# SSD chunk matrix: the scaled C.B product and its combination move from SBUF into a PSUM bank, and the ring of side banks has four instead of five

## The chip, the cores and the metric

The kernel runs on one core of one Trainium2 chip. The metric is device time in microseconds (us) of one execution. The core has five engines: PE (TensorE, matrix products), DVE (VectorE), ACT (ScalarE), POOL (GpSimd) and SP (SyncE, which here only issues DMA transfers). Each engine works through its own instructions in the order of the program; semaphores make it wait for others. SBUF is the working memory. PSUM is the memory into which PE writes; it has eight banks of 128 partitions by 512 float32.

## The reference: what is computed

Two layers are run over 256 context tokens and 1024 latent tokens, ten tiles of 128 tokens in all. In layer 0 one input projection feeds a bidirectional Mamba-2 (SSD) mixer and a convolution module. The change lies in the SSD mixer, which works in chunks of 128 tokens:

```python
acs = jnp.cumsum(dt * a_neg, axis=2)
seg = acs[:, :, :, None] - acs[:, :, None, :]
lmat = jnp.exp(jnp.where(tril[:, :, None, None], seg, -jnp.inf))
xdt = x * dt[..., None]
cb = jnp.einsum("bcign,bcjgn->bcijg", cm, bm)
y_diag = jnp.einsum("bcijg,bcijgr,bcjgrp->bcigrp", cb, lmat, xdt)
...
y_off = jnp.einsum("bcign,bcigr,bcgrpn->bcigrp", cm, jnp.exp(acs), h_in)
```

This is done forwards and backwards for 16 heads in 4 groups of 4, and the two directions are added. For each chunk and head the kernel builds one 128x128 matrix for both directions. With F and B for C.B masked to the lower and the upper triangle, it is (F times dt forward + B times dt backward) times the exponential of the decays; this matrix times x gives y_diag of both directions.

## The kernel before

**Groups.** Layer 0's SSD part is a loop over the head groups g = 0 to 3. For each, PE computes ten z tiles (the gate and dt, 264 columns) and then four conv blocks: the projections of x, B and C, followed by the 4-tap convolution (ACT evicts the bank and applies the first tap, DVE the other taps in L1146, and L1153 ends the activation). After them comes `out_first(mix["B"])`, the first half of the output projection. Matmuls of these are called main matmuls here.

**Chunk steps.** The SSD work of group g is cut into small steps (`ssd_steps`), which the object `sd` (class `Steps`) hands out between the main matmuls of the next group; those of group 3 go between the main matmuls of `out_first`. The order on every engine is thus written out ahead, by weights in a list; nothing is decided at run time but the waits.

The steps of a group are, in order:

- `prep(c)`: three transposes and C.B of chunk c on PE, copied out by ACT;
- `p1(n)`: the backward recursion. PE makes one chunk's state, POOL scales the state before (L869), DVE adds (L870);
- then for each chunk c two half-steps. `sta(c)`: `sb1(c)`, matmuls with the states (128x256) into bank b2 and with the chunk matrix (128x64) into b1; `sfw(c+1)`, the forward state of the next chunk; `sb2y(c)`, in which DVE reads b2 (L959, twice) and then b1 (L961); and `cbg(c+2)`, below. `stb(c)`: `zmul(c)` on POOL (L968 to L970), `sm(c+2)` (L923), masks on POOL (`msk`), decay arguments on DVE (`arg`, L899), and `scc(c-2)`, two transposes copied out by ACT (L988).

`cbg` builds the chunk matrix for four heads: ACT makes four exponentials (L906), then four scaled copies of the masked C.B into `cbd` (L909), and DVE adds the other direction's part in place (L912, four times 128x128). `sm` then multiplies all 512 columns with the exponentials (L923) into `Mt`, which PE reads in `sb1`. `cbd` is 512 columns of SBUF.

**PSUM banks.** `PS[0]` to `PS[7]` are the eight banks. `mm_bank()` goes round the first of them for main matmuls, `sd_bank()` round the others for the side steps. `banks(n)` sets how many the main matmuls have, and the side steps get the rest; `banks(n, a, w)` gives the side steps the w banks from `PS[a]` on. While the chunk steps run, main matmuls have three banks and side steps five, `PS[3]` to `PS[7]`. In group 0 the z tiles run with four and four, and the conv blocks that follow share the five side banks with the layer-norm steps of the convolution module (`lnb`, transposes L322 read by ACT in L716 and L729). The decay steps (`dt_chain2`) take two side banks, read by DVE in L823, L824 and L826. A bank is handed out again without asking whether it has been read; the wait for its reader follows from the order of the program.

Of the kernel before, what the change touches and what calls it, by code (L numbers as in the profile page):

```python
# [81 lines left out]
def build(tc, I, O):  # L82
    nc = tc.nc
    V, S, G, PE, SP = nc.vector, nc.scalar, nc.gpsimd, nc.tensor, nc.sync
    with ExitStack() as ctx:
# [37 lines left out]
        PS = [psall[:, i * 512:(i + 1) * 512] for i in range(8)]  # L123
# [69 lines left out]
        def banks(n, a=None, w=None):  # L193
            nmm[0] = n
            sdr[0] = (n, 8 - n) if a is None else (a, w)
# [128 lines left out]
        with tc.manual_schedule():  # L324
# [4 lines left out]
            def xa(o, n):  # L329
                return X0[:, o:o + n]  # L330
# [432 lines left out]
            tok = xa(0, 5120)  # L763
            Hb = xa(5120, 2560)
            Hf = [xa(7680 + i * 256, 256) for i in range(2)]
            cbd = xa(8192, 512)
            cbfb = xa(8704, 256)
            X2 = [xa(8960 + i * 256, 256) for i in range(2)]
            yt.append(xa(9472, 256))
# [318 lines left out]
            for g in range(4):  # L1088
# [3 lines left out]
                pend = []  # L1092
                W.need(zp[1])
                W.need(zp[1] + 1)
                banks(4 if g == 0 else 3)
                wps = [W.get(zp[0]), W.get(zp[1])]
                for t in range(NT):
                    b = mm_bank()
# [15 lines left out]
                    sd.tick(T256 * ZF)  # L1114
                    if g == 0 and t == 6:
                        sd.flush()
                banks(3)
                sd.settle()
                if g == 0:
                    lnb_pre()  # L1120
# [539 lines left out]
            for n in range(16 * 7):  # L1660
                g, j = n // 7, n % 7
# [254 lines left out]
```

## Time and profile before

| | |
|---|---|
| median of 3 runs | 2115.37 us (2112.26 to 2115.81) |
| the profiled execution | 2115.44 us, its span 2113.6 us |
| mean granted clock of PE | 0.985 |
| busy: PE, DVE, POOL, ACT | 2024.7, 1364.4, 1034.1, 941.2 us |
| middle and last chunks of groups 0, 1, 2, 3 | from 572 to 655, 710 to 792, 846 to 922 and 1005 to 1064 us |

The span runs from the first to the last instruction that the profile shows; 1.8 us of the time lies around it. Busy times overlap between engines. In rows of the profile a buffer's name is that of its pool: `ps` is a PSUM bank, `X`, `Fhi` and `Flo` are parts of SBUF. `out<-in` names what an instruction writes and reads; the number in brackets behind a row of the timeline is the idle time of its engine before it, and the instruction that ended it.

### The profile page before, as it was taken

The page shows a single profiled execution, that of the slowest core. Times are in us where ns is not written, and L with a number is a line of the kernel's source. Part 1 is how long each engine was busy: PE and PEld are TensorE (multiplying, and loading weights), DVE is VectorE, ACT ScalarE, POOL GpSimd, SP SyncE. Part 2 cuts the span into 40 slices and gives each one's busy share as a digit, 9 for nine tenths or more (in the row PEclk, how much of TensorE's full clock was granted, in tenths as well). Part 3 has the DMA queues.
Part 4 walks back from the last instruction along what each step waited for, and adds up shares of the span by engine and source line. Part 5 has one row for each costly group of instructions (what it writes and reads, how often), then busy time and mean ns, then how long its engine had stood idle before and what let it go on. Part 6 is the DMA issues. An engine that isn't in the chain of part 4 may idle for free.

```text
span 2113.6 us, 32253 instructions
## 1 busy us (share of the span) xinstructions
PE 2024.7 (96%) x12152; PEld 1792.9 (85%) x12152; DVE 1364.4 (65%) x1918; ACT 941.2 (45%) x1768; POOL 1034.1 (49%) x990
## 2 busy tenths in 40 slices
PE   7999999988989989899999999999999999989998
PEld 5778888877968869789998788889999999988987
DVE  5777888878696996985846632235555555564566
ACT  3555565557555554554644432224333333230221
POOL 3488778934554654634714422333444444435412
PEclk9999999999999999899999999999999999999999
DMA  8333321266423323334477643353223233274642
GB/s 340 108 125 130 123 100 66 88 177 191 136 80 95 100 86 103 104 115 155 146 262 228 205 135 125 110 149 112 90 92 95 96 95 95 64 254 163 200 139 81
DMA packets 177620, 283.05 MB, mean 134 GB/s; under 512 B 14432, under 2 KB 119848, under 8 KB 177464
## 3 DMA queue, kind: packets, MB, share of 16 engines
q1 hardware_dynamic: 133728, 239.12, 34.9%
q10 hardware_dynamic: 43736, 41.86, 5.8%
q8 instruction: 96, 1.57, 0.3%
q14 instruction: 60, 0.49, 0.1%
HBM read 206.30 MB, written 74.63 MB: 133 GB/s over the span
## 4 chain that ended last, share of the span: by engine, by line
PE 45%; DVE 8%; DMA 2%; POOL 2%; issue 2%; ACT 1%; ACTq 0%; SPq 0%; DVEq 0%; POOLq 0%
PE ps L207 45%; DVE X L912 2%; DVE Fhi L1146 1%; DVE Fhi L1289 1%; DVE Rl L318 1%; DVE Fhi L899 1%; ACT Rh L317 0%; DMA y2D<-Fm 0%; POOL X L863 0%; DVE Fhi L1290 0%; DVE Fhi L1288 0%; DVE Flo L683 0%; DMA Fhi<-mBD 0%; DVE Wr L259 0%; ACT Fhi L1295 0%
## 5 line engine op out<-in xcount | busy, mean ns | idle before, releaser
L207 PE MATMUL ps<-Rh,Wr 128*128 128x512 f32 (+2 forms) x2944 | 772.2, 348 | 3.1 <-ACT Rh L413 1.4
L207 PEld LDWEIGHTS ps<-Rh,Wr 128*128 128x128 f32 x2944 | 521.2, 192 | 67.4 <-issue 6.2
L207 PE MATMUL ps<-Rl,Wr 128*128 128x256 f32 x1472 | 501.2, 345 | 1.8 <-DVE Rl L415 1.7
L207 PE MATMUL ps<-Wr,Rh 128*128 128x264 f32 (+2 forms) x1812 | 411.0, 318 | 5.9 <-ACT Fhi L1108 2.3
L594 POOL TENSOR_TENSOR X<-X 128x1295 f32<-128x1295 f32 x96 | 297.3, 3097 | 77.8 <-ACT X L592 72.3
L207 PEld LDWEIGHTS ps<-Wr,Rh 128*128 128x128 f32 x1812 | 298.9, 189 | 31.3 <-ACT Fhi L1108 2.5
L207 PEld LDWEIGHTS ps<-Rl,Wr 128*128 128x128 f32 x1472 | 281.2, 192 | 29.8 <-DVE Rl L415 2.7
L207 PE MATMUL ps<-Wr,Rl 128*128 128x264 f32 (+2 forms) x946 | 300.0, 317 | 0.9 <-DVE Rl L318 0.8
L207 PEld LDWEIGHTS ps<-Wr,Rl 128*128 128x128 f32 x946 | 178.7, 189 | 14.4 <-DVE Rl L318 1.3
L207 PE MATMUL ps<-Xa,Rh 128*128 128x512 f32 (+1 forms) x582 | 172.7, 369 | 1.3 <-DVE Xa L259 0.8
L207 PE MATMUL ps<-Xb,Rh 128*128 128x512 f32 (+1 forms) x598 | 170.6, 359 | 0.1
L588 DVE SCALAR_TENSOR_TENSOR ps<-Fhi,Flo,ps 128x1295 f32<-128x1295 f32 x102 | 160.0, 1569 | 2.9
L259 DVE TENSOR_TENSOR Wr<-Flo,Wr 128x1024 fp32r<-128x1024 f32 (+1 forms) x67 | 105.2, 1577 | 54.7 <-ACT Wr L257 54.5
L207 PE MATMUL ps<-Xa,Rl 128*128 128x512 f32 (+1 forms) x342 | 127.1, 372 | 7.1 <-DVE Rl L318 7.1
L1459 ACT ACTIVATE Wr<-Flo 128x512 fp32r<-128x512 f32 x96 | 59.8, 624 | 142.8 <-PE ps L207 141.5
L207 PEld LDWEIGHTS ps<-Xa,Rh 128*128 128x128 f32 x582 | 106.1, 192 | 20.2 <-DVE Xa L259 1.1
L1460 DVE TENSOR_TENSOR Wr<-Flo,Wr 128x512 fp32r<-128x512 f32 x96 | 96.5, 1005 | 39.3 <-ACT Wr L1459 39.3
L207 PEld LDWEIGHTS ps<-Xb,Rh 128*128 128x128 f32 x598 | 105.2, 188 | 17.7 <-DVE Xb L259 0.5
L207 PE MATMUL ps<-S,Wr 128*128 128x256 f32 (+1 forms) x768 | 117.7, 309 | 0.0
L1146 DVE SCALAR_TENSOR_TENSOR Fhi<-Fhi,Flo 128x256 f32<-128x256 f32 (+2 forms) x144 | 113.7, 790 | 4.4
L207 PEld LDWEIGHTS ps<-S,Wr 128*128 128x128 f32 x768 | 110.8, 188 | 0.0
L592 ACT ACTIVATE X<-Fhi,Flo 128x1295 f32<-128x1295 f32 x78 | 103.5, 1373 | 13.4 <-ACT Fhi L641 7.5
(279 smaller groups left out, 3421.5 us busy)
## 6 DMA issues: line engine op xcount, KB each, us to landing
Fhi<-abD SPq DMA_DIRECT2D x80, 256.0 KB, 3.4
Fhi<-in_ada SPq DMA_DIRECT2D x34, 512.0 KB, 7.9
Flo<-in_wug SPq DMA_DIRECT2D x32, 512.0 KB, 4.8
Flo<-in_wB SPq DMA_DIRECT2D x24, 512.0 KB, 3.3
vD<-Flo ACTq DMA_DIRECT2D x40, 256.0 KB, 2.3
Xb<-vD SPq DMA_DIRECT2D x16, 640.0 KB, 5.1
pD<-Xb SPq DMA_DIRECT2D x32, 320.0 KB, 2.5
Flo<-in_wA SPq DMA_DIRECT2D x16, 512.0 KB, 3.5
```

What stands on the lines that cost most here:

```text
L207: PE.matmul(out=out, lhsT=a, rhs=b, start=st, stop=sp)
L259: e.tensor_tensor(out=l_, in0=r, in1=h_.bitcast(F32), op=SUB)
L318: eng.tensor_tensor(out=rl, in0=src, in1=rh.bitcast(F32), op=SUB)
L588: V.scalar_tensor_tensor(out=aD[:, 0:n], in0=u[:, k:k + n], scalar=wc(k), in1=aD[:, 0:n], op0=MULT, op1=ADD)
L592: S.activation(out=o[:, 0:n], in_=u[:, k:k + n], func=AF.Copy, scale=wc(k))
L594: G.tensor_tensor(out=aP[:, 0:n], in0=aP[:, 0:n], in1=o[:, 0:n], op=ADD)
L899: V.scalar_tensor_tensor(out=a[:, q], in0=a[:, q2], scalar=nA[:, sl(1, c)][:, h:h + 1], in1=a[:, q], op0=ADD, op1=MIN)
L912: V.scalar_tensor_tensor(out=cbd[:, q], in0=cbfb[:, 128:256], scalar=dt[:, sl(1, c)][:, h:h + 1], in1=cbd[:, q], op0=MULT, op1=ADD)
L1146: V.scalar_tensor_tensor(out=ob[:, a:e], in0=ib[:, a + k:e + k], scalar=w4(k), in1=ob[:, a:e], op0=MULT, op1=ADD)
L1289: V.tensor_tensor(out=y[:, s_], in0=y[:, s_], in1=grow[:, s_], op=MULT)
L1459: S.activation(out=w[:, 0:512], in_=src, func=AF.Copy)
L1460: V.tensor_tensor(out=w[:, 512:1024], in0=src, in1=w[:, 0:512].bitcast(F32), op=SUB)
```

## The change

`cbd` becomes `PS[7]`. While the chunk steps run, the side steps go round four banks, `PS[3]` to `PS[6]`, and the main matmuls keep their three. Group 0's z tiles keep four and four; so does everything behind the chunk steps of group 3, by a later `banks(4)`.

```diff
             Hf = [xa(7680 + i * 256, 256) for i in range(2)]
-            cbd = xa(8192, 512)
+            cbd = PS[7]
...
                 W.need(zp[1] + 1)
-                banks(4 if g == 0 else 3)
+                if g == 0:
+                    banks(4)
+                else:
+                    banks(3, 3, 4)
                 wps = [W.get(zp[0]), W.get(zp[1])]
...
                     if g == 0 and t == 6:
                         sd.flush()
-                banks(3)
+                banks(3, 3, 4)
                 sd.settle()
```

Every engine has the same instructions in the same order as before; what differs is where some of them read and write, and what they wait for. On DVE, the second half of one chunk in group 0 stood so (`X_92` and `Fhi` are SBUF, the names behind "waits" are the engines waited for):

```order
L961 TENSOR_TENSOR X_92<-X_92,ps 128x256
L912 SCALAR_TENSOR_TENSOR X_92<-X_92,Flo 128x128 [waits DVE_49,Activation_49]
L912 SCALAR_TENSOR_TENSOR X_92<-X_92,Flo 128x128 [waits Activation_49] x3
L1105 SCALAR_TENSOR_TENSOR Fhi<-Fhi,ps 128x256 [waits Activation_49]
L1111 TENSOR_TENSOR Fhi<-ps,Flo 128x2x4
L923 TENSOR_TENSOR Fhi<-Fhi,X_92 128x512 [waits DVE_49]
```

and stands now so:

```order
L961 TENSOR_TENSOR X_92<-X_92,ps 128x256
L912 SCALAR_TENSOR_TENSOR ps<-X_92,Flo,ps 128x128 [waits DVE_49,Activation_49]
L912 SCALAR_TENSOR_TENSOR ps<-X_92,Flo,ps 128x128 [waits DVE_49] x3
L1108 SCALAR_TENSOR_TENSOR Fhi<-Fhi,ps 128x256 [waits Activation_49]
L1114 TENSOR_TENSOR Fhi<-ps,Flo 128x2x4
L923 TENSOR_TENSOR Fhi<-Fhi,ps 128x512 [waits DVE_49]
```

Each of the four L912 waited for its own L909 on ACT; now the first waits for the last L909, since a wait concerns the whole bank, and the others for the L912 ahead (`DVE_49`).

On PE, at `sb1` of a middle chunk of group 1, behind the two transposes of the half-step before, it was:

```order
L322 MATMUL ps<-Flo 128x128 [waits DVE_49,Activation_49]
L322 MATMUL ps<-Flo 128x128
L207 MATMUL ps<-X_92,Fhi 128x256 [waits Activation_49]
L207 MATMUL ps<-X_92,Fhi 128x256 [waits Pool_49]
L207 MATMUL ps<-X_92,Fhi 128x64 [waits DVE_49]
```

and is now:

```order
L322 MATMUL ps<-Flo 128x128 [waits Activation_49]
L322 MATMUL ps<-Flo 128x128
L207 MATMUL ps<-X_92,Fhi 128x256 [waits DVE_49]
L207 MATMUL ps<-X_92,Fhi 128x256 [waits Pool_49]
L207 MATMUL ps<-X_92,Fhi 128x64 [waits Activation_49]
```

The wait for DVE's read of an old bank (L961) has moved from the transposes to the first matmul of the next half-step, one chunk nearer to that read.

## The prediction

> **What bounds the kernel now.** I read the engine totals first, then the stretches in which the chunk steps run, then who waits there.
>
> ```profile
> PE 2024.7 (96%) x12152; PEld 1792.9 (85%) x12152; DVE 1364.4 (65%) x1918; ACT 941.2 (45%) x1768; POOL 1034.1 (49%) x990
> PE 45%; DVE 8%; DMA 2%; POOL 2%; issue 2%; ACT 1%; ACTq 0%; SPq 0%; DVEq 0%; POOLq 0%
> ```
>
> TensorE (PE) is busy 96% of the span, and the chain that ended last is mostly PE, with VectorE (DVE) second. That is an average. The stretches of the chunk steps of head groups 0, 1, 2 and 3 read so (columns: window, its length, busy PE, PEld, DVE, ACT, POOL, granted PE clock, DMA share, GB/s):
>
> ```profile
> 571.71:654.73 83.02, 73.43 (x377) 61.44 (x376) 78.88 (x161) 49.37 (x131) 47.65 (x82) 0.94 0.28 88
> 710.25:791.70 81.45, 69.13 (x365) 59.03 (x364) 79.48 (x159) 49.37 (x131) 50.17 (x79) 0.94 0.28 88
> 845.54:921.65 76.11, 66.16 (x332) 56.91 (x331) 72.66 (x149) 43.86 (x122) 46.76 (x79) 0.89 0.31 100
> 1004.67:1063.60 58.93, 58.83 (x470) 57.55 (x469) 46.16 (x92) 34.39 (x104) 40.87 (x66) 1.00 0.46 150
> ```
>
> In the first three DVE is busy 95 to 98% and PE 85 to 88%: there DVE sets the pace. In the fourth PE is busy all the time and DVE 78%: there each microsecond for which PE stands still is a microsecond of the kernel. The change makes DVE cheaper and PE wait earlier, so the two kinds of stretch answer differently.
>
> One DVE-bound chunk of group 1 (columns: start, length, engine, line, what, count, idle before in brackets):
>
> ```profile
> 742.05 0.41 DVE L961 TENSOR_TENSOR X<-X,ps 128x256 f32<-128x256 f32 x1
> 749.29 0.68 DVE L923 TENSOR_TENSOR X<-Fhi,X 128x512 f32<-128x512 f32 x1
> 749.89 1.13 DVE L899 SCALAR_TENSOR_TENSOR Fhi<-Fhi,Flo 128x128 f32<-128x128 f32 x4
> 751.45 1.26 ACT L909 ACTIVATE X<-X,Flo 128x128 f32<-128x128 f32 x4
> 751.93 0.41 DVE L961 TENSOR_TENSOR X<-X,ps 128x256 f32<-128x256 f32 x1
> 752.09 0.72 POOL L968 TENSOR_TENSOR Fhi<-Fhi,X 128x256 f32<-128x256 f32 x1 [2.90 <-DVE Fhi L959]
> 752.26 2.79 DVE L912 SCALAR_TENSOR_TENSOR X<-X,Flo 128x128 f32<-128x128 f32 x4
> 753.70 0.73 POOL L970 TENSOR_TENSOR Fhi<-Fhi 128x256 f32<-128x256 f32 x1
> 828.64 1.16 DVE L912 SCALAR_TENSOR_TENSOR X<-X,Flo 128x128 f32<-128x128 f32 x4 [0.92 <-ACT X L909]
> ```
>
> From L961 to L961 a chunk takes 9.9 us. The pack of four L912 takes 2.79 us beside POOL's L968 to L970 (its two-input 128x256 products), and 1.16 us where POOL is free (last row, chunk 0 or 1 of group 2).
>
> **The change part by part.** No instruction is added, removed or moved. `cbd` becomes a PSUM bank, and waits go by bank; the side ring has four banks.
>
> *The pack of L912 and its readers.* The rows for the new price:
>
> ```profile
> L588 DVE SCALAR_TENSOR_TENSOR ps<-Fhi,Flo,ps 128x1295 f32<-128x1295 f32 x102 | 160.0, 1569 | 2.9
> L912 DVE SCALAR_TENSOR_TENSOR X<-X,Flo 128x128 f32<-128x128 f32 x160 | 92.5, 635 | 5.3 <-ACT X L909 3.6 <-issue 1.6
> L923 DVE TENSOR_TENSOR Fhi<-Fhi,X 128x512 f32<-128x512 f32 x20 | 15.6, 782 | 0.4
> L1288 DVE TENSOR_TENSOR Fhi<-ps,Fhi 128x512 f32<-128x512 f32 x18 | 12.3, 681 | 0.9 <-PE ps L207 0.9
> L1552 DVE SCALAR_TENSOR_TENSOR Flo<-ps,Flo 128x128 f32<-128x128 f32 x16 | 5.6, 351 | 31.5 <-PE ps L207 31.4
> L588 DVE SCALAR_TENSOR_TENSOR ps<-Fhi,Flo,ps x102: 1554/1572/1574, 66.8 to 426.5; 128x1295 f32<-128x1295 f32 x102
> 182.61 4.77 DVE L588 SCALAR_TENSOR_TENSOR ps<-X,Flo,ps 128x1295 f32<-128x1295 f32 x3
> ```
>
> One 128x128 operation with a PSUM input takes 0.351 us (L1552). Afterwards each L912 reads and writes the bank that the one ahead wrote, so it waits for it. L588 accumulates in PSUM in the same way: three take 4.77 us, that is (4.77 - 1.569) / 2 = 1.60 us apart, 0.03 more than one lasts. So a pack becomes 4 x 0.351 + 3 x 0.03 = 1.50 us, whatever POOL does (L588 runs 1554 to 1574 ns throughout). The mean pack was 4 x 0.635 = 2.54 us, so 1.04 us is saved on the mean, 1.29 in the chunk above, while packs like the one at 828.64 lose 0.34. L923 goes from 0.78 towards 0.68: 0.1 more.
>
> The Trainium skill (VectorE: DVE Perf Modes, "The DRAIN you can't avoid") says that a semaphore between chained operations costs nothing. The rows differ: four unchained L899 take 1.13 us, four chained ones would take about 1.5. By that rule a pack would stay near 1.16 us, 0.34 less, and the sum below would come out 21 x 0.34 = 7 us lower, at the edge of the second rival.
>
> Against the saving stands a wait. Now the first L912 starts after the first L909; afterwards it waits for the fourth, since all four write one bank, and those wait for each other too:
>
> ```profile
> 794.02 0.60 ACT L1134 ACTIVATE Fhi<-ps 128x512 f32<-128x512 f32 x1 [2.15 <-PE ps L207]
> 794.66 0.81 ACT L1142 ACTIVATE Fhi<-Fhi,Flo 128x513 f32<-128x513 f32 x1
> L909 ACT ACTIVATE X<-X,Flo 128x128 f32<-128x128 f32 x160 | 50.6, 387 | 0.0
> ```
>
> One L909 takes 0.387 us; L1142 reads what L1134 writes and starts 0.04 us after its end (794.62 to 794.66). No ACT row here writes PSUM; I take 0.387 for that too. The pack of L909 goes from 1.26 to 3 x 0.43 + 0.39 = 1.67 us, so in the chunk above it ends at 753.12, and DVE, ready at 752.26, stands 0.86 us. I count this for half the packs, 0.4 us on the mean; ends: 0 (ACT always early) and 0.9 (never). Some of POOL's blocking also moves on to the next DVE operation with two SBUF inputs: 0.2. So a chunk saves 1.04 + 0.1 - 0.4 - 0.2 = 0.55 us of DVE. About seven chunks a group lie in the DVE-bound stretch: 7 x 3 x 0.55 = 11.5 us. Ends: 0 and 24 (all of 1.14).
>
> *The ring of four in groups 0 to 2.* Each chunk takes two banks in its first half-step, and in the second half-step one for its transposes. With five, the matmuls of the next first half-step (`sb1`, 128x256) find a bank long read; with four they reuse the bank that L961 of the chunk before reads. PE against that L961:
>
> ```profile
> 726.49 1.03 PE L207 MATMUL ps<-X,Fhi 128*128 128x256 f32 x4
> 730.40 0.41 DVE L961 TENSOR_TENSOR X<-X,ps 128x256 f32<-128x256 f32 x1
> 734.45 1.87 PE L207 MATMUL ps<-X,Fhi 128*128 128x256 f32 x12
> 742.86 1.03 PE L207 MATMUL ps<-X,Fhi 128*128 128x256 f32 x4
> 750.02 2.93 PE L207 MATMUL ps<-X 128*128 128x64 f32 x10 [6.13 <-DVE X L923]
> ```
>
> PE comes to `sb1` at 726.49, 734.45 and 742.86; it would have to wait for L961 until 730.81, 742.46 and 752.34, so 4.3, 8.0 and 9.5 us. Queued behind are the main matmuls of the conv blocks. Yet DVE needs nothing of PE from that time until its next L959, and so goes on; and PE already waits here for DVE, 6.13 us for L923 at 750.02. What is lost is PE's lead: the wait that ended at 750.02 ends at 752.34, and 1.03 us of `sb1` comes after it, 3.4 us in all, once a group. Walking PE through the three stretches, each chunk starting at the later of PE's own end and DVE's L961 as the trace has them, and the last matmuls behind the decay step's reads of its bank, leaves PE 6.5, 2.9 and 5.2 us late at the ends, 14.6 together. Ends: 0 (DVE's work is all that counts) and 3 x 8. With the 11.5 saved, groups 0 to 2 come to +3.1 us.
>
> *The backward recursion before the chunks* takes one bank a step (`p1`) and adds it in L870. With four banks step n waits for L870 of step n-2, behind POOL's product:
>
> ```profile
> 677.82 0.60 PE L207 MATMUL ps<-X 128*128 128x256 f32 x2
> 680.68 0.42 DVE L870 TENSOR_TENSOR X<-X,ps 128x256 f32<-128x256 f32 x1 [3.72 <-POOL X L869]
> ```
>
> In group 1 PE would stand 3.3 us, from 677.8 to 681.1. In the others the same comparison gives 0.7 to 0.8 each: +5.6. DVE waits there itself, so nothing covers it. Ends: 0 and 7.
>
> *Group 3*, where PE is the bound:
>
> ```profile
> 1019.85 1.03 PE L207 MATMUL ps<-X,Fhi 128*128 128x256 f32 x4
> 1022.75 0.41 DVE L961 TENSOR_TENSOR X<-X,ps 128x256 f32<-128x256 f32 x1
> 1060.14 1.88 PE L207 MATMUL ps<-X,Fhi 128*128 128x256 f32 x12
> 1060.86 0.41 DVE L961 TENSOR_TENSOR X<-X,ps 128x256 f32<-128x256 f32 x1
> ```
>
> The first such wait is 1023.16 - 1019.85 = 3.3 us; it shifts PE behind DVE, so the next ones shrink below zero, until the last adds 1.1: +4.4. Ends: 1 and 9.
>
> *The layer-norm transposes in group 0* take side banks too, and come to their reader one use earlier:
>
> ```profile
> 483.36 0.60 PE L322 MATMUL ps<-Flo,X 128*128 128x128 f32 x4
> 486.37 1.97 PE L322 MATMUL ps<-Flo,X 128*128 128x128 f32 x16 [2.41 <-DVE Flo L824]
> ```
>
> The four at 483.36 move behind L824's end at 486.3, which costs their 0.6 us, since PE waits there anyway; two or three such places: +1.5. Ends: 0 and 4.
>
> *Given back.* PE idles later on work that doesn't come from this change:
>
> ```profile
> 939.00:985.00 46.00, 41.56 (x311) 38.81 (x310) 17.02 (x22) 21.55 (x38) 13.45 (x22) 0.96 0.56 172
> ```
>
> Of the 4.4 us idle here I let 3 absorb delay: -3. Ends: 0 and -4.4.
>
> Sum: 3.1 + 5.6 + 4.4 + 1.5 - 3 = +11.6. Against the profiled execution of 2115.44 us (0.07 above the median of the runs, 2115.37) this makes 2127 us.
>
> **The rivals.**
>
> *Faster.* The saving is whole and PE's lead doesn't count: L909 is early enough, POOL's blocking vanishes, PE always catches up before DVE needs it. Then 24 us less DVE work in groups 0 to 2, against 5.6 + 4.4 + 1.5 for the other waits: -12.5, 2103 us; with two thirds of the saving 2111. It decides from about 0.95 us saved a chunk on. For it speaks DVE's 95 to 98%; against it the pack at 828.64, where DVE stood 0.92 us for the first L909 alone.
>
> *No change.* Waits only change their place: the small first waits are absorbed and lost lead equals saved DVE work, 2115, give or take 4.
>
> By the Trainium skill's rule on semaphores (VectorE: DVE Perf Modes, above) the time would be 2120, just beside this case.
>
> *Worse by the clock.* A wait of PE is followed by a stretch at half clock:
>
> ```profile
> 747.75:754.58 6.83, 4.56 (x19) 4.38 (x20) 6.73 (x18) 4.29 (x12) 3.78 (x7) 0.50 0.32 96
> ```
>
> After the 6.13 us wait the granted clock is 0.50 for 6.8 us, which is up to 3.4 us of PE work lost. If the longer waits of 8 to 9.5 us bring four or five more such stretches, or those waits reach PE-bound places, 12 to 16 us come on top: 2141. Against it: the long waits were there before, under another name.
>
> **How the numbers follow.** The forecast (2120 to 2133) 0.44, faster 0.25 (2103 to 2111), no change 0.17, worse by the clock 0.14. A difference under 0.2%, 4 us, is about what a measurement of this kernel can't tell from none. Faster 0.25, same 0.17, slower 0.44 + 0.14 = 0.58. For 8 in 10 the range leaves out the outer half of the faster case and the outer part of the last: 2107 to 2142.
>
> **What the profile after would show.** Right, if the L912 pack takes about 1.5 us in every chunk (wrong, if near 1.2 or above 2) with an idle time before it ended by ACT's L909; if in the list of waits PE's longest are for DVE's L961 instead of L923; if PE's `p1` matmuls wait for L870 in group 1 for about 3 us; and if the PE busy share of group 3's stretch falls below 95%. If in groups 0 to 2 the stretch from the first to the last chunk is over 5 us shorter each, the lead didn't count and the forecast is wrong towards faster; if more than the present half-clock stretches stand there, wrong towards slower.

## The result, and the profile after

The changed kernel takes 2132.53 us in the median (2127.3 to 2135.49, 6 runs) against 2114.69 us before (2112.26 to 2116.98, 6 runs): a ratio of 1.0084, 95% interval [1.0073, 1.0095]. It is 17.8 us slower; 2127 with a range of 2107 to 2142 was forecast. The profiled execution took 2131.94 us, its span is 2130.1 us, 16.5 more than before.

The engine totals after, then the windows between the L961 of chunk 1 and of chunk 9 of each group, which answer to the four shown of before (columns as there):

```profile
PE 2031.9 (95%) x12152; PEld 1797.4 (84%) x12152; DVE 1325.9 (62%) x1918; ACT 950.0 (45%) x1768; POOL 1022.1 (48%) x990
574.46:652.48 78.02, 71.23 (x367) 61.21 (x366) 70.41 (x161) 49.94 (x128) 45.22 (x81) 0.93 0.30 95
717.91:794.65 76.74, 67.29 (x359) 57.51 (x358) 71.84 (x158) 50.04 (x127) 45.77 (x78) 0.96 0.31 98
853.66:929.93 76.27, 63.28 (x318) 53.65 (x317) 64.83 (x149) 44.92 (x120) 45.55 (x79) 0.89 0.32 101
1014.12:1079.62 65.50, 61.16 (x460) 59.03 (x459) 37.64 (x93) 36.16 (x104) 38.28 (x67) 0.95 0.45 142
```

DVE is 38.5 us less busy, and the kernel is slower all the same. The window's ends cut the span into pieces, and the difference of each piece says where the time went:

| piece (by the ends of L961) | before | after | difference |
|---|---|---|---|
| start to group 0, chunk 1 | 571.71 | 574.46 | +2.8 |
| group 0, chunks 1 to 9 | 83.02 | 78.02 | -5.0 |
| from there to group 1, chunk 1 | 55.52 | 65.43 | +9.9 |
| group 1, chunks 1 to 9 | 81.45 | 76.74 | -4.7 |
| to group 2, chunk 1 | 53.84 | 59.01 | +5.2 |
| group 2, chunks 1 to 9 | 76.11 | 76.27 | +0.2 |
| to group 3, chunk 1 | 83.02 | 84.19 | +1.2 |
| group 3, chunks 1 to 9 | 58.93 | 65.50 | +6.6 |
| from there to the end | 1050.00 | 1050.48 | +0.5 |

Two of the three DVE-bound stretches became shorter, by 4.7 to 5.0 us; that of group 2 did not. The loss lies between the stretches, where the backward recursion and the first chunks run, and in group 3.

The head of the list of what PE waited for from 530 to 1090 us (engine, what it was about to do, what released it: total us, times, longest):

```profile
PE ps L207 <- DVE X L961: 23.8, 10, 4.5
PE ps L322 <- DVE Flo L824: 4.8, 1, 4.8
PE ps L207 <- DVE X L870: 4.7, 6, 2.9
PE ps L207 <- DVE X L923: 3.7, 3, 1.6
```

Before, L923 led this list; now it is L961, and L870 is new. The groups of the pack (busy us, mean ns, idle us before, and what ended it):

```profile
L909 ACT ACTIVATE ps<-X,Flo 128x128 f32<-128x128 f32 x160 | 58.7, 367 | 3.9
L912 DVE SCALAR_TENSOR_TENSOR ps<-X,Flo,ps 128x128 f32<-128x128 f32 x160 | 56.8, 355 | 28.7 <-ACT ps L909 17.8 <-issue 6.5
```

One L912 fell from 635 to 355 ns, whatever POOL does, but DVE's idle time ahead of them rose from 5.3 to 28.7 us: of 35.7 us saved, 23.4 went back into a wait. Two long waits in places where PE sets the pace, each with the window of 7 us that follows (columns as above):

```profile
680.86 1.22 PE L207 MATMUL ps<-X 128*128 128x256 f32 x2 [2.91 <-DVE X L870]
680.00:687.00 7.00, 6.14 (x26) 5.96 (x27) 1.26 (x3) 0.00 (x0) 2.69 (x5) 0.51 0.50 152
1032.24 2.07 PE L207 MATMUL ps<-X,Fhi 128*128 128x256 f32 x4 [3.21 <-DVE X L961]
1031.50:1038.50 7.00, 6.26 (x23) 5.72 (x24) 5.75 (x16) 4.69 (x14) 5.61 (x11) 0.52 0.46 137
```

These are in the recursion of group 1 and at chunk 4 of group 3. After 2.91 and 3.21 us of idle PE the granted clock stands at 0.51 and 0.52 for 7 us. Before, both places ran at full clock.

### The profile page after: what moved, and what is told of

Same layout as the page of the kernel before. It is cut to its first block, busy times and chain, and to the rows that moved or that the text cites. A ratio compares the mean times of both kernels' runs of the same rounds, so it can differ in the third digit from the quotient of the medians.

```text
span 2130.1 us, 32182 instructions
## 1 busy us (share of the span) xinstructions
PE 2031.9 (95%) x12152; PEld 1797.4 (84%) x12152; DVE 1325.9 (62%) x1918; ACT 950.0 (45%) x1768; POOL 1022.1 (48%) x990
## 4 chain that ended last, share of the span: by engine, by line
PE 47%; DVE 6%; DMA 2%; ACT 2%; issue 2%; POOL 1%; ACTq 0%; SPq 0%; DVEq 0%; POOLq 0%
PE ps L207 46%; DVE Fhi L1292 1%; DMA Flo<-in_wout0a 1%; DVE Fhi L1149 1%; DVE ps L912 1%; DVE Rl L318 1%; DVE Fhi L899 1%; ACT Rh L317 0%; ACT ps L909 0%; DVE Fhi L1293 0%; DVE Fhi L1291 0%; PE ps L322 0%; DVE Flo L683 0%; DVE Wr L259 0%; ACT Fhi L1298 0%
## 5 line engine op out<-in xcount | busy, mean ns | idle before, releaser
L207 PEld LDWEIGHTS ps<-Wr,Rl 128*128 128x128 f32 x946 | 180.2, 190 | 15.5 <-DVE Rl L318 2.5
```

The costliest lines, as they stand in the source:

```text
L207: PE.matmul(out=out, lhsT=a, rhs=b, start=st, stop=sp)
```

## The experiments

All are edits of the changed kernel, or of the one before where that is said; the diffs show what differs. Theory A: the ring of four is the loss, and the PSUM copy a gain that doesn't pay for it. Rival B: the packs, chained in one bank, are the loss. Rival C: the ring costs in the recursion and in group 3 alone, and PE's lead is worth nothing in the DVE-bound stretches.

| kernel | median us | ratio to before, 95% interval |
|---|---|---|
| ring of four alone (cbd in SBUF) | 2135.55 | 1.0100 [1.0086, 1.0114] |
| five banks until the chunks | 2123.46 | 1.0040 [1.0026, 1.0054] |
| two main banks, cbd in PSUM | 2110.80 | 0.9978 [0.9968, 0.9987] |
| two main banks, cbd in SBUF | 2116.09 | 1.0004 [0.9995, 1.0013] |
| copies first | 2111.45 | 0.9992 [0.9983, 1.0000] |
| before, copies first | 2113.22 | 0.9995 [0.9985, 1.0004] |
| two main banks, copies first | 2089.27 | 0.9882 [0.9869, 0.9895] |
| two main banks only in the chunks, copies first | 2092.58 | 0.9896 [0.9883, 0.9909] |
| five banks until the chunks, copies first | 2104.77 | 0.9956 [0.9944, 0.9968] |
| b2 first | 2125.76 | 1.0054 [1.0040, 1.0069] |
| kept warm, first try | 2133.64 | 1.0101 [1.0086, 1.0115] |
| kept warm, second try | 2124.08 | 1.0052 [1.0038, 1.0065] |

The pieces of six of them, each as the difference to the kernel before in us, from one profiled execution each ("best" is two main banks, copies first):

| piece | ring alone | five until chunks | two main, SBUF | two main, PSUM | five, copies first | best |
|---|---|---|---|---|---|---|
| start to group 0, chunk 1 | +2.4 | +1.8 | +0.9 | -0.2 | -0.1 | -3.1 |
| group 0, chunks 1 to 9 | +0.2 | -5.3 | +0.1 | -5.3 | -5.8 | -5.3 |
| to group 1, chunk 1 | +5.8 | +3.2 | +0.3 | +2.6 | -0.5 | -1.6 |
| group 1, chunks 1 to 9 | +0.6 | -4.3 | 0.0 | -4.8 | -5.8 | -6.3 |
| to group 2, chunk 1 | +1.7 | +4.3 | +0.1 | +4.3 | -0.1 | -1.5 |
| group 2, chunks 1 to 9 | +5.0 | -0.3 | 0.0 | -4.9 | -0.6 | -5.7 |
| to group 3, chunk 1 | -0.9 | +1.2 | 0.0 | +1.6 | -3.6 | -3.0 |
| group 3, chunks 1 to 9 | +6.4 | +6.4 | +1.4 | +3.0 | +7.6 | +1.6 |
| from there to the end | -0.8 | -1.5 | -1.1 | -0.2 | -1.9 | -1.4 |

**The ring alone.**

```diff
-            cbd = PS[7]
+            cbd = xa(8192, 512)
```

> The changed kernel with cbd back in SBUF, but the ring of four side banks kept (PS[7] unused). Theory A, the ring's earlier waits are the loss and the PSUM copy is a gain that pays part of it: then this kernel is slower than the changed one. Recursion and group 3 cost the same as in the changed kernel (+11 and +8 us), the first three stretches of chunk steps lose PE's lead without the shorter packs (about +10 to +15): 2140 to 2147 us. Rival B, the chained packs of L909 and L912 in one PSUM bank are the loss: 2113 to 2119 us. Rival C, PE's lead is worth nothing in the DVE-bound stretches, but the ring costs in the recursion and in group 3: about 2132, as the changed kernel.

It is the slowest of all, 3 us above the changed kernel. So the ring is the loss (about +20), and B is out as the main cause. It came out 4.5 us below A's range and 3.6 above rival C's 2132, so the median doesn't tell these two apart. The windows of its four stretches:

```profile
574.10:657.30 83.20, 74.09 (x376) 63.08 (x375) 79.07 (x161) 49.41 (x130) 47.54 (x82) 0.92 0.28 87
718.60:800.70 82.10, 72.03 (x361) 61.15 (x360) 79.93 (x159) 49.04 (x130) 48.82 (x79) 0.90 0.28 89
856.30:937.40 81.10, 67.06 (x320) 56.51 (x319) 72.82 (x148) 43.13 (x120) 46.37 (x79) 0.85 0.29 93
1019.50:1084.80 65.30, 61.08 (x466) 59.13 (x465) 46.01 (x92) 34.59 (x103) 41.61 (x67) 0.95 0.44 138
```

The DVE-bound stretches of groups 0 and 1 last about as long as before (83.02 and 81.45): the waits of PE cost next to nothing there. That of group 2 takes 5.0 us more (76.11 before), and DVE is busy for 90% of it instead of 95%. Near its end DVE now waits twice for the late PE, 4.8 us together; before, it did not wait for PE in that stretch:

```profile
928.77 0.42 DVE L959 TENSOR_TENSOR X<-ps,Flo 128x256 f32<-128x256 f32 x1 [3.12 <-PE ps L207]
936.30 0.42 DVE L959 TENSOR_TENSOR X<-ps,Flo 128x256 f32<-128x256 f32 x1 [1.72 <-PE ps L207]
```

So PE's lead is worth something, and rival C leaves this out; why it runs out in group 2 alone stays open. The way to group 1's chunk 1 takes 718.6 - 657.3 = 61.3 us against 55.5, but that is the recursion: PE waits 3.3 us for one L870, and 3.4 us at a granted clock of 0.50 follow, which is some 1.7 us of PE's work by estimate.

**Five banks where cbd isn't alive.** The ring goes to four only ahead of the first chunk half-step.

```diff
-                st.append((1.0, lambda: stb(-3)))
+                st.append((1.0, lambda: (four(), stb(-3))))
...
+            def four():
+                started[0] = True
+                sdr[0] = (3, 4)
...
-                    banks(3, 3, 4)
+                    banks(3)
...
```

> The changed kernel, but the ring has five banks through the conv blocks of group 0 and each backward recursion, and goes to four only where the first chunk half-step begins and PS[7] is first written as cbd. Theory A: the waits of p1 for L870 go, and with them the half-clock stretch behind the longest (680 to 687 us): -7 in group 1, -2 each in groups 2 and 3, so 2120 to 2124 us, and no wait of p1 for L870 over 0.7 us. Rival B (chained packs are the loss): 2130 to 2134, since nothing of the packs changes.

9 us are back, as A has it. What PE waited for from 660 to 712 us, in the changed kernel (first two) and here (last two):

```profile
PE ps L207 <- DVE X L870: 3.2, 2, 2.9
PE ps L207 <- DVE X L923: 1.1, 1, 1.1
```

```profile
PE ps L207 <- DVE X L923: 1.1, 1, 1.1
PE ps L322 <- ACT Fhi L981: 0.9, 1, 0.9
```

The wait for L870 is gone, and no half-clock stretch stands there. The way to group 1's chunk 1 takes 58.7 us: 6.7 less than in the changed kernel, still 3.2 more than before. Most of that rest isn't lost lead: 2.6 us of it stand there with five side banks throughout as well (two main banks, cbd in PSUM), and none with four banks in the chunk steps and the copies first (table). It belongs to the loop of the copies, below.

**Two main banks.** The bank for cbd is taken from the main matmuls instead; the second kernel is its control.

```diff
-                    banks(3, 3, 4)
+                    banks(2, 2, 5)
...
-                banks(3, 3, 4)
+                banks(2, 2, 5)
```

> The changed kernel with cbd in PS[7] and five side banks again (PS[2] to PS[6]), the main matmuls going round two banks instead of three in the same places. To be read against the next kernel, which differs only in cbd. Theory A: it is faster than that one by what the shorter packs save where PE keeps its lead, 8 to 18 us over groups 0 to 2. Rival B: slower than that one, by about 15 us. What two main banks cost is open: 0 to 30 us over the kernel before.

> The control of the kernel ahead: cbd in SBUF, five side banks (PS[2] to PS[6]), two main banks, PS[7] unused. Against the kernel before it shows what two main banks cost alone: 0 to 30 us. Theory A: 8 to 18 us above the kernel with cbd in PSUM. Rival B: below it.

The control can't be told from the kernel before: the main matmuls didn't need their third bank. With cbd in PSUM 5.3 us are gained, less than A's 8 to 18. With the ring whole all three DVE-bound stretches are shorter than before, by 5.3, 4.8 and 4.9 us, group 2's too. But the pieces ahead of them are longer, and ate the saving: L912's idle time was still 27.8 us.

**The copies first.** That idle is the wait of the first L912 for the fourth L909. Nothing of the copies depends on the exponentials, so ACT can make them first; in kernels with this order L906 is the copies' line and L909 the exponentials'.

```diff
                 def cbg(c):
                     a = AB[c % 2]
+                    for h in range(4):
+                        q = slice(h * 128, (h + 1) * 128)
+                        S.activation(out=cbd[:, q], in_=cbfb[:, 0:128], func=AF.Copy, scale=...)
                     for h in range(4):
                         ...
                         S.activation(out=a[:, q2], in_=a[:, q], func=AF.Exp, ...)
-                    for h in range(4):
-                        q = slice(h * 128, (h + 1) * 128)
-                        S.activation(out=cbd[:, q], in_=cbfb[:, 0:128], func=AF.Copy, scale=...)
```

> The changed kernel, with ACT's four scaled copies (L909) ahead of its four exponentials (L906) in each chunk. Theory A: the pack of L912 loses time since its first waits for the fourth copy (L912's idle time before it is 28.7 us in the changed kernel, 5.3 before). With the copies first this idle falls under 12 us and the time to 2122 to 2129 us. Rival: DVE meets the wait one step on, at L923, which then waits for the later exponentials, or PE's waits for L961 hold the pace anyway: 2130 to 2134.

The gain is 21 us, twice the most that A had it at. The group of L912, and two of its packs in the first half-steps of group 1, first of before, then of the changed kernel, then here:

```profile
692.90 1.16 DVE L912 SCALAR_TENSOR_TENSOR X<-X,Flo 128x128 f32<-128x128 f32 x4 [0.89 <-ACT X L909]
698.00 1.18 DVE L912 SCALAR_TENSOR_TENSOR X<-X,Flo 128x128 f32<-128x128 f32 x4 [0.54 <-issue]
```

```profile
700.26 1.53 DVE L912 SCALAR_TENSOR_TENSOR ps<-X,Flo,ps 128x128 f32<-128x128 f32 x4 [2.07 <-ACT ps L909]
706.32 1.53 DVE L912 SCALAR_TENSOR_TENSOR ps<-X,Flo,ps 128x128 f32<-128x128 f32 x4 [1.72 <-issue]
```

```profile
L912 DVE SCALAR_TENSOR_TENSOR ps<-X,Flo,ps 128x128 f32<-128x128 f32 x160 | 56.6, 354 | 4.3
689.46 1.53 DVE L912 SCALAR_TENSOR_TENSOR ps<-X,Flo,ps 128x128 f32<-128x128 f32 x4
693.75 1.53 DVE L912 SCALAR_TENSOR_TENSOR ps<-X,Flo,ps 128x128 f32<-128x128 f32 x4
```

In the first half-steps nothing fills DVE, and each turn is a loop through two engines: arguments (L899), exponentials, copies, L912, L923, the next arguments. The loop takes 5.10 us before, 6.06 in the changed kernel and 4.29 here, where the copies run beside L923 and L899. Ahead of the first three packs of each group L912 stands idle for 18.1 us in all in the changed kernel, against 5.3 before and nothing here. Of the 20.6 us between the two profiled executions 20.4 lie in the four pieces ahead of the stretches.

Whether this order is worth as much without the PSUM bank:

> The kernel before (cbd in SBUF, five side banks, three main banks) with the scaled copies ahead of the exponentials. It tells whether the 21 us that this order was worth in the changed kernel belong to the PSUM bank. Theory A (the bank-wide wait made the copies stand between exponentials and L912): with cbd in SBUF L912 waits only 5.3 us in all, so little is to be had: 2107 to 2114 us. Rival D (the copies' place is worth as much in SBUF, since ACT no longer waits for DVE's L899 ahead of them): 2092 to 2098 us.

It isn't: 1.4 us, within the noise. Rival D is out, and the wait belongs to the bank.

With two main banks as well:

> cbd in PS[7], five side banks, two main banks, and the scaled copies ahead of the exponentials. The kernel without the last took 2110.8 us. Theory A: the shorter idle of L912 is saved on DVE where DVE sets the pace: 2100 to 2107 us. Rival (the wait moves to L923): 2109 to 2113.

> As the kernel ahead, but the main matmuls keep three banks (and the side steps PS[3] to PS[7]) until the first chunk half-step, and go to two (side steps PS[2] to PS[6]) only from there. The waits of PE for L1114, the last reader of a z tile's bank (8.1 us with two main banks), should mostly go: 2 to 6 us below the kernel ahead. If PE makes these up later, within 1 us of it.

2089.27 us, against 2113.88 for the kernel before beside it: 24.6 us or 1.2% less, and below the range that was expected. It is the best of all. Keeping the third main bank until the chunks adds nothing: 3.3 us more instead of 2 to 6 less. Its control, SBUF with both, wasn't run; with SBUF each of the two edits alone is worth 0 within about 0.1%. The windows of the best kernel in groups 1 and 3:

```profile
700.20:775.40 75.20, 69.70 (x370) 59.56 (x370) 71.76 (x159) 49.70 (x129) 48.71 (x79) 0.95 0.30 97
978.20:1038.70 60.50, 60.50 (x483) 59.32 (x483) 37.49 (x92) 35.30 (x102) 37.31 (x66) 1.00 0.46 146
```

Group 1's stretch is 6.3 us shorter than before, and in group 3 PE is busy without a gap.

> The changed kernel with five side banks through each backward recursion and with the copies first: both mends together. If they are independent (9 and 21 us), 2100 to 2105 us. The waits of the chunk steps for L961 stay, so it should stay above the kernel with two main banks and copies first (2089.3); how far above is what the ring of four costs in the chunk steps alone: 8 to 15 us.

2104.77: the two mends add up (9 and 21 expected apart, 27.8 together). The 15.5 us to the best kernel are about what four side banks instead of five still cost in the chunk steps (the pair also differs in the main banks, three against two): by the table 5.1 us in group 2's stretch and 6.0 in group 3's. Another 3.0 lie ahead of group 0's chunk 1, a piece that moves by some 2 us without any edit there (see below).

**b2 first.**

```diff
-                    b1, b2 = sd_bank(), sd_bank()
+                    b2, b1 = sd_bank(), sd_bank()
```

> The changed kernel with the two banks of sb1 handed out in the other order: b2 first. The 128x256 matmuls then get a bank long read, and the 128x64 ones the bank b2 of the chunk before, which L959 reads just ahead of L961. If what counts is PE's place behind DVE, only the 1 us of the first matmuls and the 0.4 us of L961 are won, once a group: 2127 to 2132 us. If a bank more or less decides by itself, nothing: 2132.

6.8 us are won, a little more than the range, with as many banks. PE's waits there now name the read ahead of L961:

```profile
PE ps L207 <- DVE Fhi L959: 8.7, 4, 3.6
PE ps L207 <- DVE Flo L959: 7.2, 3, 3.3
```

In group 3's stretch, 2.1 us shorter than in the changed kernel, PE now waits 2.0 us where it waited 3.21. So with as many banks the price also hangs on which read a bank waits for, but this is shown for those 2.1 us alone. Another 2.3 lie on the way to group 1's chunk 1, where PE's wait for L870 is as long as it was (3.07 us) and only the stretch at half clock behind it is shorter, 3.4 us; and 2.1 lie behind the chunk steps.

**Kept warm.** Extra matmuls of constants, whose results nobody uses, fill the two long waits (the remarks behind `#` are explanations). The added lines shift the line numbers behind them: L990 below is L981 elsewhere.

```diff
+                    if g == 1 and n == 2:
+                        warm()                  # three 128x512 matmuls into a main bank
                     mm(bk[:, 0:256], tk(c)[:, 256:384], XP[n % 3], True, True)
...
+                    if g == 3 and c == 4:
+                        for _ in range(6):      # first try: warm()
+                            mm(b1[:, 0:256], ident, cols[:, 0:256], True, True)
```

> The changed kernel with three extra 128x512 matmuls of constants into a main bank ahead of two matmuls that wait long: p1 step 2 of group 1 (wait for L870, 2.9 us) and sb1 of chunk 4 of group 3 (wait for L961, 3.2 us). Their results aren't used. In the changed kernel each of these waits is followed by 7 us at half clock, in a stretch where PE sets the pace. If the clock is what doubles the price of the wait, both half-clock stretches go and with them up to 3.4 us each: 2126 to 2130 us. If the wait alone costs, or the clock falls anyway, the time stays at 2131 to 2134, or rises by what the extra matmuls take beyond the wait.

> As the kernel with extra matmuls in the two long waits, but those of group 3 (six of 128x256) now go into b1, which is free there, instead of a main bank, for which they had to wait themselves. In the first try the stretch at 680 us ran at full clock and group 1's first chunk came 2 us earlier. If the clock is what doubles the price of the wait: full clock in group 3 as well, its stretch of chunk steps 3 us shorter than the changed kernel's 65.5 us, and 2125 to 2130 us. If not: 2131 to 2135.

In the first try the extra matmuls of group 3 had to wait for their own bank; the clock fell there all the same, and the time stayed:

```profile
1032.29 2.07 PE L207 MATMUL ps<-Flo 128*128 128x512 f32 x2 [3.32 <-ACT Flo L990]
```

In the second try the clock was kept in both places (windows 676 to 683 and 1028 to 1035):

```profile
676.00:683.00 7.00, 6.34 (x38) 4.75 (x37) 1.36 (x4) 0.63 (x2) 2.95 (x5) 1.00 0.63 206
1028.00:1035.00 7.00, 6.83 (x53) 6.68 (x54) 5.71 (x16) 4.68 (x15) 6.05 (x11) 1.00 0.46 130
```

The time fell to 2124.08 us, though the matmul that waits for L870 still starts 3.4 us after the gap begins, 2.74 of them filled. Of the 8.4 us about 4.5 lie in these places by the profile: 2.5 on the way to group 1's chunk 1, 2.0 in group 3's stretch (63.5 against 65.5). In that profile 2.2 us were already saved by group 0's chunk 1, and 2.1 more behind the chunk steps, where nothing was changed; that part stays unexplained, and the size is known only to some 3 us.

The wait by itself doesn't settle the clock. The wait for L870 in group 1 was 2.91 us in the changed kernel and 6.8 us at half clock followed. With 3.33 us (ring alone) and 3.07 us (b2 first) only 3.4 us followed, and with the copies first none, after 3.06 us:

```profile
674.95 0.70 PE L207 MATMUL ps<-X 128*128 128x256 f32 x2 [3.06 <-DVE X L870]
675.00:682.00 7.00, 6.69 (x48) 6.19 (x49) 1.76 (x5) 2.17 (x4) 4.08 (x8) 1.00 0.42 140
```

What else decides it, these runs don't show, and part of what the second try won may be this.

The Trainium skill (TensorE: Matmul & The Clock Gate, "What's actually happening") says that the array falls to half rate after an idle window of about 3.4 us. The trace agrees in kind; the waits that brought it here were somewhat shorter, 2.91 and 3.21 us.

## Why the prediction was right, point by point

- *The price of the pack*: 1.50 us forecast, 1.53 measured in every chunk, and 355 ns for one L912 against 351. Right. By the Trainium skill's rule on semaphores (VectorE: DVE Perf Modes, "The DRAIN you can't avoid") it would be near 1.16; the trace doesn't bear that out.
- *What it saves in the stretches*: 11.5 us forecast for three groups. With the ring whole 15.0 are measured (5.3, 4.8 and 4.9), so the way was right and the size somewhat low. In the changed kernel groups 0 and 1 keep 5.0 and 4.7; in group 2 the ring, 5.0 us longer by itself, takes all of it back.
- *The wait for the fourth copy* is the step that was mis-sized. It was charged with 0.4 us for the seven chunks in a DVE-bound stretch only; there it took about 0.2 (six waits of some 0.7 us in 21 chunks). The first half-steps of each group weren't charged at all, though the quoted pack at 828.64 stood there; the loop through ACT and DVE grew by 0.96 us in the turn quoted above, and putting the copies first was worth 21 us. So the PSUM copy gave 3 us (2135.55 to 2132.53), not 11.5. The wait by the whole bank that causes it is also the rule of the Trainium skill (PSUM — Partial Sum Buffer, "PSUM bank collisions raise a hardware error": guard by bank).
- *The ring*: 14.6 + 5.6 + 4.4 + 1.5 - 3 = 23.1 us forecast, about 20.6 measured alone; the sum fits, its terms do not. The lost lead was put at 6.5, 2.9 and 5.2 us for groups 0, 1 and 2, at the ends of the stretches. Two pairs in the table differ in the ring of the chunk steps (and in the main banks): five until chunks against two main banks in PSUM, and five with copies first against the best. By them group 0 costs 0.6 to 0.7 us with the piece behind it, group 1 0.5 to 1.8, group 2 4.1 to 4.5: 5 to 7 us instead of 14.6. In groups 0 and 1 DVE did go on, as argued, but little was lost afterwards; in group 2 DVE itself had to wait for PE at L959, inside the stretch, against the argument.
- *Recursion and group 3*: 5.6 us (3.3 of them in group 1) and 4.4 forecast; five banks until the chunks, in group 0's conv blocks too, won 9 back, and group 3's stretch is 6.4 us longer with the ring alone. Both long waits were followed by 7 us at half clock. That was put down as a rival, on top of the forecast, and was half a case: it came behind the two new long waits in PE-bound places, while in the three DVE-bound stretches the mean clock, 0.93, 0.96 and 0.89, is much what it was (0.94, 0.94, 0.89).
- *Given back, 3 us of idle around 939 to 985*: between group 2 and group 3's chunk 1 only 1.2 us were lost, although that group's recursion waits too, so something was probably given back; its size wasn't measured by itself.

The saving was taken too large, and the recursion and group 3 too small, the clock among them; the lost lead was too large by 8 to 9 us and hid most of that. That the sum came within 5.5 us of the result is in part luck.

The signs named ahead stood there: packs of 1.53 us with idle time ended by L909, L961 at the head of PE's waits, 2.91 us for L870 in group 1's recursion, and PE busy for 61.16 of 65.50 us, 93%, in group 3. Of the signs against, more stretches at half clock in groups 0 to 2 came true by number only: seven instead of six, but 34.1 us together instead of 37.5.

## What to carry to other kernels

A wait on a PSUM bank concerns the whole bank: when a tile written piece by piece moves there, look for the loop in which the reader's first piece now waits for the writer's last, and make the writer early. When a bank must be found, take it from the ring whose reuse isn't waited for; three main banks and two took the same time here, five side banks and four differed by 20 us. A wait of PE is priced by the place: next to nothing where another engine sets the pace and doesn't come to wait for PE in turn (groups 0 and 1; in group 2 it did), its length where PE is the bound itself, and up to about twice that where the clock falls behind it, which it didn't each time.

## What the runs showed of the hardware

A 128x128 two-input DVE operation of 635 ns on the mean (SBUF inputs, beside POOL) takes 355 ns with one input and the output in PSUM, even though each waits for the one ahead. ACT wrote its scaled copies to PSUM in 367 ns against 387 ns to SBUF. The clock fell for 7 us after 2.91 us without a matmul, and stayed at 1.00 with 2.74 us of unused matmuls in that gap; it also stayed at 1.00 after 3.06 us without any in another kernel.
